# A transformer block on one core: h, the convolution's norm and its swish in half tiles, with the gate dots, diagonal blocks and last store rearranged

## The chip, the cores and the metric

One core of a Trainium2 chip runs the whole block as one program. The metric is device time in microseconds from launch to end. TensorE (PE) does the matrix products, VectorE (DVE) and ScalarE (ACT) the elementwise work, GpSimd (POOL) a little of it, and SyncE (SP) issues most transfers between the chip's memory and the on-chip buffer SBUF; POOL issues the rest. PE writes its results into eight banks of a second buffer, PSUM. Each engine works through its own queue in a fixed order; engines wait for one another through semaphores.

## The reference

One layer on a sequence of 1024 positions with 1024 channels, in float32:

```python
h = rmsnorm(x, pre_mix_g) * (1.0 + sc1) + sh1          # sh, sc, ga: rows of silu(c) @ ada_w + ada_b
proj = h @ w_in                                        # 1024 -> 1024 (glu) + 1536 (q, k, v) + 2048 (gates)
u = u_val * sigmoid(u_gate)
u = causal_depthwise_conv(u, conv_w, conv_b)           # 31 taps, 512 channels
u = silu(layernorm(u, conv_ln_g, conv_ln_b))
y_conv = u @ w_conv_out
y_att = stick_breaking_attention(q, k, v) @ w_att_out  # 8 heads of 64, strictly causal
merged = sigmoid(g_conv) * y_conv + sigmoid(g_att) * y_att
x = x + ga1 * rmsnorm(merged @ w_o, post_mix_g)
h = rmsnorm(x, pre_ffn_g) * (1.0 + sc2) + sh2
gate, up = split(h @ w_ffn_in)
x = x + ga2 * rmsnorm((silu(gate) * up) @ w_ffn_out, post_ffn_g)
```

## The kernel before

Activations are kept with channels on the 128 partitions and positions along the row, so a matrix of 1024 x 1024 is eight tiles of 128 x 1024. A product in full precision is made from three products of rounded parts: each operand is split into hi (rounded) and lo (the remainder), and PE computes hi·hi + hi·lo + lo·hi. The hi part is an ACT copy, the lo part a DVE subtraction. PSUM banks hold 128 x 512, so the positions are worked in two column halves, c = 0 and 1 (the slices hs).

The program runs through these stages.

*Start.* x is normed and modulated to h; its 16 tiles hhi and hlo (pool hp, 16 slots of 128 x 1024) are written by hi_op and lo_op. The order of ACT and DVE here is written out by hand (pin).

*Attention.* Four calls of attend, each for two heads. head works in blocks of 256 positions, four to a head (c from 0 to 3). For each it makes scores z on PE, sigmoids on ACT (ka, be), a product scan along the row on DVE, then transposes the probabilities on PE into the bank tr, four of 128 x 128 per bank. In a diagonal block (jp == c) one of the four is zero, and a tile of zeros is transposed for it. ACT copies tr into ahi, DVE makes alo, and PE multiplies both with v. The heads have a higher priority; other work fills PE's queue between their steps: the projections for q, k and v, the gated input of the convolution (glu, which writes u, a tile with one slot, and stores it to v_d), and the convolution (conv, which loads v_d into ph, makes 40 small products into the banks pcv, and stores to u_d).

*Gates.* Two of the eight pairs of gate tiles are plain products (the list PLAIN, four products). For the other six (GPAIRS) the product is made by a scheme with seven instead of eight half-size products. It needs sums and differences of quarters of h, the forms T1 to T4, built from f = hhi + hlo; B11, B21 and B22 are quarters of h itself. Two of a pair's seven products need only B11 and B21 and are made first, into the banks k1 and k2, stored as e_d and s_d (tiles e); other_five makes the other five.

*Norm.* ln_all loads u_d into cr, four tiles that take slots of hp, and does the layer norm over 512 channels, one column half after the other; then sigmoid, scaling and product give csil, which is split into chi and clo.

*Merge.* y_conv multiplies chi, clo with w_conv_out and with the gate. Beside it ada2_dots loads sixteen rows of the conditioning matrix and dots each with cb on DVE (dot_c). Then the attention's output, o_d, goes through w_att_out and its gate, the two branches are added, and the sum is split into mhi and mlo.

*Output projection, feed-forward, end.* These follow, and only the last step of them is touched: finish, called for the last quarter with last = ka, multiplies by the root rs and the gate, adds x1 (tiles xr) and stores four tiles.

A scheduler orders the instructions of each engine by priority and by its own estimate of times; tc.high_priority(offset) raises the priority of what stands in it. A tile of a pool waits for the former holder of its slot. The functions load and store issue the transfer on SP's and on POOL's queue. gemm is a product over banks of both column halves, load_w loads and splits a weight tile, banks2 takes two of the three banks of the pool main, and bkg takes turns over seven banks.

Of the kernel before, what the change touches and what calls it, by code (L numbers as in the profile page):

```python
# [18 lines left out]
P = 128  # L19
D = 1024  # L20
# [25 lines left out]
LN_PRI = 100  # L46
LN_DVE0 = (0, 1)
# [28 lines left out]
def tile_block(ctx: ExitStack, tc: tile.TileContext, xT, vecs, ada1, ada2, win, wv, wcv, wat, wo, w1, w2, cvw, out):  # L76
# [8 lines left out]
    hp = mkpool(ctx, "hp", 16)  # L85
# [125 lines left out]
    with ExitStack() as s0:  # L211
# [100 lines left out]
        def hi_op(k, cols=slice(0, T)):  # L312
            act.activation(hhi[k][:, cols], xs[k][:, cols], AF.Identity, bias=shift_of(k), scale=1.0)

        def lo_op(k):
            dve.scalar_tensor_tensor(hlo[k], xs[k], shift_of(k), hhi[k], op0=ALU.add, op1=ALU.subtract)
# [17 lines left out]
        for k in range(KT):  # L334
            hhi.append(hp.tile([P, T], F32R, tag="act", name=f"hhi{k}"))
            hlo.append(hp.tile([P, T], F32R, tag="act", name=f"hlo{k}"))
# [81 lines left out]
    with ExitStack() as sC:  # L418
        pc = mkpool(sC, "pc")
        with ExitStack() as sA:  # L420
# [25 lines left out]
            def conv(ct):  # L446
# [4 lines left out]
                for hf in range(2):  # L451
# [15 lines left out]
                    load(u_d[ct][hf * (NG // 2):(hf + 1) * (NG // 2)].rearrange("g p m -> p g m"), o)  # L467
# [53 lines left out]

            def head(p, hh, qst, kst, klo, vts, oT):
# [6 lines left out]
                for ci, c in enumerate(order):  # L529
# [5 lines left out]
                    for sc in range(nsc - 1, -1, -1):  # L535
# [27 lines left out]
                        for jp in range(min(c, 2 * sc + 1), 2 * sc - 1, -1):  # L563
                            tr = pst.tile([P, CH], F32, tag="tr", name=f"tr{tag}_{c}_{jp}")
                            for jj in range(2):
                                j = 2 * jp + jj
                                for ii in range(2):
                                    jo = (j - 4 * sc) * P
                                    src = zeros if (jp == c and jj == 1 and ii == 0) else probs[ii][:, jo:jo + P]
                                    o = jj * 256 + ii * P  # L570
                                    pe.transpose(tr[:, o:o + P], src, ident)  # L571
                            ahi = pa.tile([P, CH], F32R, tag="ahi", name=f"ahi{tag}_{c}_{jp}", bufs=2)
                            alo = pa.tile([P, CH], F32R, tag="alo", name=f"alo{tag}_{c}_{jp}", bufs=2)
                            act.activation(ahi, tr, AF.Copy)  # L574
                            dve.tensor_tensor(alo, tr, ahi, op=ALU.subtract)  # L575
                            for jj in range(2):
                                j = 2 * jp + jj
                                lhs = vts[j][:, hidx].rearrange("p a d -> p (a d)")
                                cols = slice(jj * 256, jj * 256 + 256)
# [22 lines left out]
            v = v_half(0)  # L602
            for p in range(4):
                glu(p)
                if p == 2:
                    v = v_half(1)
# [3 lines left out]
            conv(3)  # L610
# [1180 lines left out]
```

## Time and profile before

| | us |
|---|---|
| median of 3 runs | 1417.07 (1415.29 to 1421.37) |
| profiled execution | 1416.81 |
| its span, first to last instruction | 1415.0 |
| PE busy | 1383.6 |
| DVE busy | 1060.4 |
| ACT busy | 651.3 |
| POOL busy | 96.7 |

The span is the time from the first to the last instruction that the profiler saw; the run's time has a little on both sides of it. "Busy" is the time in which at least one instruction of the engine was under way. In a row of the profile, a line number such as L571 is that of the kernel before as printed above; "out<-in" are the names of tiles without their numbers; and an entry in square brackets is the idle time of the engine ahead of that instruction, with what ended it. In a row of waits the three numbers are the total in us, how often, and the longest. In a row of a group of instructions they stand as count, busy us, mean ns of one, and idle us ahead of them. In a row of transfers they are count, size, and the median time from issue to landing.

### The profile page before, as it was taken

What the parts mean: (1) busy time and instruction counts of PE and PEld (TensorE: products, weight loads), DVE (VectorE), ACT (ScalarE), POOL (GpSimd) and SP (SyncE); (2) the same over time, 40 slices, a digit from 0 to 9 for tenths busy, and PEclk for the clock granted to TensorE, in tenths of its full rate; (3) what the DMA queues carried; (4) which work ended last, traced back from release to release, by engine and by line L of the source; (5) the groups of instructions that cost most, each with busy time, mean ns of one, the idle gap of its engine ahead of it and who ended that gap; (6) DMA issues with size and microseconds to landing.
All of it is one profiled execution on the core that took longest, in us unless ns stands there. A gap on an engine that the chain in (4) does not pass through costs nothing.

```text
span 1415.0 us, 18809 instructions
## 1 busy us (share of the span) xinstructions
PE 1383.6 (98%) x6886; PEld 1156.1 (82%) x6886; DVE 1060.4 (75%) x1602; ACT 651.3 (46%) x1136; POOL 96.7 (7%) x183
## 2 busy tenths in 40 slices
PE   7999999999999999999999999999999999999996
PEld 4798898898888878888877778888888887888886
DVE  6898598576767789779588878778877775775357
ACT  5375465364553447412356553334444453334441
POOL 0000000000001110000012100001111110000000
PEclk8999999999999999999999999999999999999998
DMA  9112041131253645784935545456777769588833
GB/s 382 74 37 75 30 141 54 45 114 66 77 177 111 228 179 175 280 277 137 361 120 173 185 147 173 157 173 228 242 255 246 259 245 392 170 333 280 281 116 119
DMA packets 91116, 258.73 MB, mean 183 GB/s; under 512 B 9744, under 2 KB 20112, under 8 KB 90000
## 3 DMA queue, kind: packets, MB, share of 16 engines
q1 hardware_dynamic: 75088, 202.99, 42.1%
q0 software_dynamic: 15936, 54.54, 10.3%
q8 instruction: 54, 0.88, 0.3%
q14 instruction: 38, 0.31, 0.1%
HBM read 190.91 MB, written 66.58 MB: 182 GB/s over the span
## 4 chain that ended last, share of the span: by engine, by line
PE 80%; DVE 6%; issue 6%; DMA 5%; ACT 2%; POOL 1%; SPq 0%; DVEq 0%; POOLq 0%; ACTq 0%
PE ka L958 12%; PE ka L1500 8%; PE kc L958 7%; PE pwo L881 6%; PE pb L1500 4%; PE pgv L180 3%; PE pg L180 3%; PE pyc L180 3%; PE pya L180 3%; PE pv L481 3%; PE pcv L461 3%; PE tr L571 2%; PE pq L180 2%; PE pgg L180 2%; PE pk L180 2%
## 5 line engine op out<-in xcount | busy, mean ns | idle before, releaser
L559 DVE TENSOR_TENSOR_SCAN ka<-ka 128x128 f32<-128x128 f32 (+2 forms) x96 | 91.4, 968 | 22.8 <-ACT ka L555 22.5
L555 ACT ACTIVATE ka<-z 128x128 f32<-128x128 f32 (+2 forms) x96 | 47.1, 496 | 58.8 <-PE z L554 34.4
L575 DVE TENSOR_TENSOR alo<-tr,ahi 128x512 fp32r<-128x512 f32 x80 | 53.2, 685 | 18.2 <-ACT ahi L574 17.5
L1500 PE MATMUL ka<-gt,w2f 128*128 128x512 f32 x264 | 63.4, 390 | 0.8 <-DMA w2f<-w_d 0.8
L574 ACT ACTIVATE ahi<-tr 128x512 fp32r<-128x512 f32 x80 | 46.3, 601 | 38.1 <-PE tr L571 25.8
L561 DVE TENSOR_TENSOR be<-be,ka 128x127 f32<-128x127 f32 (+2 forms) x96 | 53.4, 573 | 9.6 <-ACT be L556 4.9
L1500 PEld LDWEIGHTS ka<-gt,w2f 128*128 128x128 f32 x264 | 49.4, 188 | 11.5 <-issue 1.4
L1066 PE MATMUL ke<-b,w_hi 128*128 128x512 f32 x176 | 55.2, 394 | 0.0
L135 DVE SCALAR_TENSOR_TENSOR ada<-ada,cb 128x1024 f32<-128x1024 f32 x32 | 38.8, 1223 | 20.7 <-DMA ada<-in_ada_dram 20.6
L556 ACT ACTIVATE be<-z 128x128 f32<-128x128 f32 (+2 forms) x96 | 46.2, 495 | 9.5 <-PE tr L571 9.3
L571 PE MATMUL tr<-ident,be 128*128 128x128 f32 x288 | 47.8, 273 | 0.4 <-DVE alo L575 0.4
L580 PE MATMUL av<-ahi,vst 128*128 128x256 f32 x160 | 44.2, 292 | 0.0
L461 PE MATMUL pcv<-ph,cvw 128*128 128x128 f32 x320 | 42.5, 276 | 0.8 <-DMA ph<-v_d 0.8
L581 PE MATMUL av<-alo,vst 128*128 128x256 f32 x160 | 42.8, 293 | 0.0
L461 PEld LDWEIGHTS pcv<-ph,cvw 128*128 128x128 f32 x320 | 39.5, 192 | 1.5 <-issue 1.2
L1066 PEld LDWEIGHTS ke<-b,w_hi 128*128 128x128 f32 x176 | 33.0, 188 | 7.8 <-issue 1.0
L481 PE MATMUL pv<-wv_hi,hhi 128*128 128x256 f32 x128 | 36.8, 288 | 2.1 <-DVE qst L505 1.4
L159 ACT ACTIVATE gt<-X 128x512 fp32r<-128x512 f32 x33 | 20.4, 630 | 39.5 <-DVE X L1543 12.4
L481 PE MATMUL pv<-wv_hi,hlo 128*128 128x256 f32 x128 | 36.7, 287 | 0.0
L481 PE MATMUL pv<-wv_lo,hhi 128*128 128x256 f32 x128 | 36.4, 285 | 0.0
L551 PE MATMUL z<-kst,qst 128*128 128x256 f32 (+2 forms) x96 | 36.2, 382 | 0.0
L571 PEld LDWEIGHTS tr<-ident,be 128*128 128x128 f32 x288 | 34.7, 140 | 1.8 <-PE z L554 0.5
(533 smaller groups left out, 4097.7 us busy)
## 6 DMA issues: line engine op xcount, KB each, us to landing
w_d<-w2o POOLq DMA_DIRECT2D x44, 512.0 KB, 8.0
w2f<-w_d SPq DMA_DIRECT2D x44, 512.0 KB, 5.4
ada<-in_ada_dram SPq DMA_DIRECT2D x32, 512.0 KB, 6.1
w2r<-in_w_dram SPq DMA_DIRECT2D x44, 256.0 KB, 3.8
w1g<-in_w_dram SPq DMA_DIRECT2D x21, 512.0 KB, 3.6
w1u<-in_w_dram SPq DMA_DIRECT2D x21, 512.0 KB, 5.2
cvw<-in_cvw_dram SPq DMA_DIRECT2D x20, 512.0 KB, 3.7
ada_w<-in_ada_dram SPq DMA_DIRECT2D x8, 1024.0 KB, 12.0
```

Of the source, the lines that this page charges most:

```text
L180: pe.matmul(bank, st[:, cols], mv[k][:, c * CH:(c + 1) * CH], start=(i == 0 and s == 0), stop=(i == n - 1 and s == 2))
L461: pe.matmul(cv[:, gi * TM:(gi + 1) * TM], wts[n][:, at:at + P], ph[:, g, SH - 1 - d:SH - 1 - d + TM], start=(d == 0), stop=(d == SH - 1))
L481: pe.matmul(pv[:, :256], st[k][:, tcols], mv[:, wc], start=(k == 0 and i == 0), stop=(k == KT - 1 and i == 2))
L555: act.activation(kap[:, s_lo:s_hi], z[:, zo:zo + w], AF.Sigmoid, bias=0.0, scale=-0.125)
L559: dve.tensor_tensor_scan(rev, rev, rev, init, op0=ALU.mult, op1=ALU.bypass)
L561: dve.tensor_tensor(beta[:, :m], beta[:, :m], kap[:, s_lo + 1:s_lo + 1 + m], op=ALU.mult)
L571: pe.transpose(tr[:, o:o + P], src, ident)
L575: dve.tensor_tensor(alo, tr, ahi, op=ALU.subtract)
L881: pe.matmul(bank_, st[:, cols], mv[k][:, cs], start=(k == 0 and q == 0), stop=(k == KT - 1 and q == 2))
L958: pe.matmul(bank_, st[:, cols], t[:, mv], start=(first and j == 0 and s == 0), stop=(j == HK - 1 and s == 2), skip_group_check=not first)
L1066: pe.matmul(kbs[f], wes[f][st][:, cols], t[:, mv], start=(i == 0 and j == 0 and q == 0), stop=(j == HK - 1 and q == 2), skip_group_check=i ...
L1500: pe.matmul(dst, w[st][:, cols], g[mv], start=first and s == 0, stop=last and s == 2, skip_group_check=more)
```

## The change

The change has these parts.

- h, in place of 16 tiles of 128 x 1024, is written as 32 half tiles of 128 x 512 in three kinds of slots: the second column half of its first four channel tiles (kind 0, 8 slots), the first column half of these (kind 1, 8 slots), and both halves of the other four (kind 2, 16 slots). hi_op, lo_op and the building of f work in halves.
- The norm of column half c (ln_half) takes slots of kind c, with priorities 1000 and 600; it stands behind the gates in the program, and before them by its priority. Swish, chi and clo are half tiles too; clo takes slots of kind 2. After y_conv the slots are given back, and 16 whole ones are opened for the merge.
- The early products of the gate pairs are made for two pairs at a time, and B21's accumulates in the bank of B11's; the DVE addition between them goes.
- In a diagonal block three transposes are made, not four. The zero quarter lies in two pairs of tiles (diag_t) that are set to zero once; the order of the quarters is turned so that the zero one comes first.
- The sixteen dots of ada2_dots go from y_conv into attention: 6, 5 and 5 behind the first three calls of glu, each loaded on POOL's queue into the slot of u.
- conv stores to u_d on POOL's queue, and the last conv stands behind the first plain gate.
- The last tile of the merge is worked in column halves at a raised priority (LASTM).
- In the last call of finish, ACT copies three of four tiles of x1 into PSUM ahead, POOL does one of the four output tiles, DVE works on pairs of rows at once, and the stores go out in the order 2, 3, 0, 1, pinned.

```diff
+    def half(kind, name, dt=F32):
+        return hq.tile([P, CH], dt, tag=f"half{kind}", name=name, bufs=(8, 8, 16)[kind])
...
         def lo_op(k):
-            dve.scalar_tensor_tensor(hlo[k], xs[k], shift_of(k), hhi[k], op0=ALU.add, op1=ALU.subtract)
+            for cs in hs:
+                dve.scalar_tensor_tensor(hlo[k][:, cs], xs[k][:, cs], shift_of(k), hhi[k][:, cs], op0=ALU.add,
+                                         op1=ALU.subtract)
...
-            hhi.append(hp.tile([P, T], F32R, tag="act", name=f"hhi{k}"))
-            hlo.append(hp.tile([P, T], F32R, tag="act", name=f"hlo{k}"))
+            kind = (1, 0) if k < KT // 2 else (2, 2)
+            hhi.append(halves(kind, f"hhi{k}", F32R))
+            hlo.append(halves(kind, f"hlo{k}", F32R))
...
-                    load(u_d[ct][hf * (NG // 2):(hf + 1) * (NG // 2)].rearrange("g p m -> p g m"), o)
+                    store(u_d[ct][hf * (NG // 2):(hf + 1) * (NG // 2)].rearrange("g p m -> p g m"), o)
...
+                                    if on and jj == 1 and ii == 0:
+                                        continue
...
+                            if on:
+                                ahi, alo = diag_t[next(ndiag) % 2]
+                                used = slice(P, CH)
...
+            def ada2_dots(n):
+                for _ in range(n):
+                    col = a2.popleft()
+                    w = pc.tile([P, D], F32, tag="u", name=f"ada2_{col}", bufs=1)
+                    store(w, ada2[col - 2 * KT])
+                    dot_c(w, cb, col)
+
             for p in range(4):
                 glu(p)
+                ada2_dots((6, 5, 5, 0)[p])
...
-            conv(3)
             for n in PLAIN:
+                if n == PLAIN[1]:
+                    conv(3)
...
+            for i0 in range(0, len(GPAIRS), 2):
+                two = GPAIRS[i0:i0 + 2]
+                ek, a12 = {}, {}
+                for i in two:
+                    raw = wp.tile([P, T], F32, tag="wraw", name=f"ew{i}")
+                    load(raw, win[20 + 2 * i])
+                    ek[i] = bank(f"k1_{i}")
+                    prod0(ek[i], w_op(f"a11_{i}", raw[:, :CH], act, dve), "B11")
+                    a12[i] = w_op(f"a12_{i}", raw[:, CH:], act, dve)
+                    e0 = sgp.tile([P, CH], F32, tag="sg", name=f"ee0_{i}", bufs=2)
+                    act.activation(e0, ek[i], AF.Copy)
+                    store(e_d0[i], e0)
+                for i in two:
+                    prod0(ek[i], a12[i], "B21", False)
+                    e1 = sgp.tile([P, CH], F32, tag="sg", name=f"ee1_{i}", bufs=2)
+                    act.activation(e1, ek[i], AF.Sigmoid, bias=0.0, scale=1.0)
+                    store(s_d[2 * i][:, :CH], e1)
...
+        def ln_half(c):
+            s0_, s1_, mean, sq = (half(c, f"l{nm}{c}") for nm in ("s0", "s1", "mean", "sq"))
+            cr = [half(c, f"cr{ct}_{c}") for ct in range(CONVT)]
+            for ct in range(CONVT):
+                load(cr[ct], channels(u_d[ct])[:, c * CH:(c + 1) * CH])
+            dve.tensor_tensor(s0_, cr[0], cr[1], op=ALU.add)
...
+                for oh in range(NCH):
+                    ms = slice(oh * mh, (oh + 1) * mh)
+                    dve.tensor_tensor(o.t[oh].rearrange("p (m r) -> p r m", r=PH)[:, c * r2:(c + 1) * r2],
+                                      ar[:, :, ms], sr[:, :, ms], op=ALU.mult)
...
-            if q == LN_AT:
-                with tc.high_priority(offset=LN_PRI):
-                    ln_all()
+        cr = {}
+        for c, prio in ((0, 1000), (1, 600)):
+            with tc.high_priority(offset=prio):
+                cr[c] = ln_half(c)
+        with tc.high_priority(offset=300):
+            csl = [halves((c, c), f"csil{ct}") for c in range(NCH) for ct in (2 * c, 2 * c + 1)]
+            for ct in range(CONVT):
+                silu(ct, cr, csl[ct])
...
+            if last:
+                xp = {}
+                for mm_ in (2, 3, 1):
+                    xp[mm_] = bank(f"x1p{mm_}").rearrange("p (a b) -> p a b", a=2)
+                    act.activation(xp[mm_], xrs[c, mm_][:, :, cols], AF.Copy)
             rstd_from(rs, m, a, ps_sum, D)
+            if last:
...
+                pool.tensor_tensor(y0, y0, r2, op=ALU.mult)
+                pool.tensor_tensor(y0, y0, xrs[c, 0][:, :, cols], op=ALU.add)
+                for m, y in ((2, y2_), (3, y3)):
+                    for i in range(2):
+                        dve.scalar_tensor_tensor(y[:, i], last[2 * (m - 2) + i][:, cols],
+                                                 gpost2[:, 2 * m + i:2 * m + i + 1], rs, op0=ALU.mult, op1=ALU.mult)
+                    add(dve, y, y, xp[m])
+                    put(m, y)
+                dve.tensor_tensor(y1, y1, r2, op=ALU.mult)
+                add(dve, y1, y1, xp[1])
+                put(0, y0)
+                put(1, y1)
```

171 lines of the change are left out of this document (94 added, 77 removed).

## The prediction

> **What bounds the kernel now.** I read the page first, then the sums over stretches of time, then PE's waits, then single moments.
>
> ```profile
> span 1415.0 us, 18809 instructions
> PE 1383.6 (98%) x6886; PEld 1156.1 (82%) x6886; DVE 1060.4 (75%) x1602; ACT 651.3 (46%) x1136; POOL 96.7 (7%) x183
> PE 80%; DVE 6%; issue 6%; DMA 5%; ACT 2%; POOL 1%; SPq 0%; DVEq 0%; POOLq 0%; ACTq 0%
> ```
>
> The profiled execution took 1416.81 us, 1.81 us more than its span and 0.26 us less than the median 1417.07 of the three runs. PE is busy for 98% of the span: whatever does not shorten PE's own work, its gaps, or the end after its last matmul moves nothing. Stage by stage (attention; gates with the convolution's norm; merge):
>
> ```profile
> core 0: us, PE busy (x) PEld busy (x) DVE busy (x) ACT busy (x) POOL busy (x), PEclk, DMA share, GB/s
> 107.00:432.00 325.00, 323.87 (x2019) 284.43 (x2018) 231.65 (x326) 172.41 (x355) 7.13 (x7) 1.00 0.28 88
> 457.00:513.00 56.00, 54.56 (x235) 43.43 (x233) 41.44 (x66) 26.78 (x49) 8.64 (x16) 1.00 0.62 211
> 513.00:570.00 57.00, 56.10 (x240) 44.94 (x241) 54.55 (x81) 39.23 (x54) 6.00 (x12) 1.00 0.53 180
> 588.00:666.00 78.00, 78.00 (x346) 64.61 (x345) 66.45 (x98) 17.17 (x17) 0.54 (x1) 1.00 0.68 233
> ```
>
> In attention PE lacks 1.13 us of 325, in the merge nothing; in the gates 1.44 and 0.90 us, while DVE is at 54.55 of 57 in the second gate stretch. PE's waits between 350 and 600 us are these six, 3.6 us together:
>
> ```profile
> PE ka L415 <- DVE gv L703: 1.2, 1, 1.2
> PE kc L415 <- DVE gw L705: 0.8, 1, 0.8
> PE pcv L461 <- DMA ph<-v_d: 0.8, 1, 0.8
> PE tr L571 <- DVE alo L575: 0.4, 1, 0.4
> PE kc L415 <- DVE s1o L402: 0.2, 1, 0.2
> PE ka L415 <- DVE s2o L402: 0.2, 1, 0.2
> ```
>
> A wait costs a little more than its gap. Matmuls of 512 columns start 78.00 / 346 = 0.225 us apart (the merge's row above), so behind the two of the first row below the next was due at 511.85 + 0.45 = 512.30. It starts at 513.70: 1.40 us lost for a gap shown as 1.16, part of it the first matmul's longer start. I add 0.17 us to each wait.
>
> ```profile
> 511.85 0.68 PE L415 MATMUL kc<-T1o,s1o 128*128 128x512 f32 x2
> 513.70 3.06 PE L415 MATMUL ka<-T3o,s3o 128*128 128x512 f32 x12 [1.16 <-DVE gv L703]
> ```
>
> **The change, part by part.**
>
> *Diagonal transposes.* Each of the 8 heads has 4 diagonal blocks, each with one transpose of zeros; the change takes these 32 out and lets two kept tiles hold the zeros.
>
> ```profile
> L571 PE MATMUL tr<-ident,zeros x32: 270/273/279, 84.9 to 417.6; 128*128 128x128 f32 x32
> 404.19 0.27 PE L571 MATMUL tr<-ident,zeros 128*128 128x128 f32 x1
> 404.30 0.71 PE L571 MATMUL tr<-ident,be 128*128 128x128 f32 x5
> ```
>
> 273 ns is the time through the array; what one occupies is the distance to the next start, 404.30 - 404.19 = 0.11 us. 32 x 0.11 = 3.5 us off an engine that lacks 1.13 us of its stage: -3.5. ACT's and DVE's ops on these blocks also shrink from 512 to 384 columns; neither is on the path, so 0.
>
> *conv(3) behind the first plain gate.* PE waited 0.8 us for the convolution's input, ph. With a gate of 48 matmuls (48 x 0.23 = 11 us) ahead of it the load has landed: -(0.8 + 0.17) = -1.0. Its stores go from SP's queue to POOL's; POOL is busy 7.13 us in 325, so 0. If the gate runs dry elsewhere the 1.0 stays: ends 0 and -1.0.
>
> *Gates and norm.* The four remaining DVE waits are 1.2 + 0.8 + 0.2 + 0.2 = 2.4 us, with 4 x 0.17 = 3.1 us. What is DVE doing when PE waits? It waits itself, for the norm's loads, with gate work queued behind:
>
> ```profile
> 497.21 0.69 DVE L734 TENSOR_TENSOR la<-cr,cr 128x512 f32<-128x512 f32 x1 [3.88 <-DMA cr<-u_d]
> 499.76 0.69 DVE L736 TENSOR_TENSOR la<-la,cr 128x512 f32<-128x512 f32 x1 [1.26 <-DMA cr<-u_d]
> ACT ee L629 <- DVE ee L628: 17.7, 5, 7.6
> ```
>
> Before, the slots for cr come free only when the early gate products have read h's first column half. The half norm takes slots of the second half, which nothing reads after the B-forms are built, so its loads go out tens of us earlier and DVE does some 17 of its 512-wide ops (17 x 0.61 = 10 us, step from the L741 row below) in a stretch where it is at 41.44 of 56. The early products' two halves accumulate in one bank, which drops 6 DVE adds (L628) and ACT's 17.7 us of waits for them. So I take all of it: -3.1; ends 0 and -3.1. The swish on DVE, already strided, keeps its element count:
>
> ```profile
> L760 DVE TENSOR_TENSOR csil<-cr,csig 128x1024 f32<-128x1024 f32 x4 | 8.7, 2178 | 0.0
> ```
>
> 16 quarters of 0.54 us make the same 8.7 us: 0.
>
> *h in halves at the start.* The lo op is split eight times; at 0.69 us for 512 columns against
>
> ```profile
> L316 DVE SCALAR_TENSOR_TENSOR hlo<-x,mod,hhi x8: 1278/1280/1283, 28.2 to 59.7; 128x1024 fp32r<-128x1024 f32 x8
> ```
>
> that is at most 8 x (2 x 0.69 - 1.28) = 0.8 us more DVE work, while the first half is ready 0.6 us sooner. Ends +0.8 and -0.6, taken as 0.
>
> *The sixteen gate dots.* They go from the merge into attention, and their loads from SP's queue to POOL's, through the single slot of u.
>
> ```profile
> L135 DVE SCALAR_TENSOR_TENSOR ada<-ada,cb 128x1024 f32<-128x1024 f32 x16 | 19.3, 1222 | 6.9 <-DMA ada<-in_ada_dram 6.9
> DVE ka L559 <- ACT ka L555: 21.0, 20, 2.9
> DVE alo L575 <- ACT ahi L574: 17.0, 12, 5.8
> ```
>
> In the merge their leaving frees 19.3 us of DVE, worth 0, since PE misses nothing there; for the same reason the finer last merge step is 0. In attention DVE rises from 231.65 to 251 of 325. A dot waits in DVE's queue for its load (6.9 us over 16, here), and behind it wait scans and products of the heads. Ends: 0, if other PE work covers it, and +6.9, if none does. Two rows alone hold 38 us of DVE waits in the same stage, against which PE lost 1.13 us, so I take a value near the covered end: +1.2, a sixth.
>
> The Trainium skill, page "DMA: Bandwidth & Descriptors", section "Anatomy of one DMA", fits a POOL-issued transfer as 2.0 us plus bytes over 436 GB/s: an estimate of 3.2 us for these 512 KB, and by it the dots would find their data and the term would be 0. The rows further down (6.1 and 8.0 us) speak for the longer time, so the sum keeps +1.2.
>
> *The end.* rs is ready at 1405.8; then DVE works alone:
>
> ```profile
> 1405.83 1.43 DVE L1637 TENSOR_TENSOR yc<-yc,frs 128x256 f32<-128x256 f32 x4
> 1407.18 1.65 DVE L1640 SCALAR_TENSOR_TENSOR yc<-ka,gpost,frs 128x256 f32<-128x256 f32 x4
> 1408.75 2.76 DVE L1540 TENSOR_TENSOR yc<-yc,xr 128x256 f32<-128x256 f32 x8
> 506.95 2.49 DVE L741 TENSOR_TENSOR cr<-cr,lm 128x512 f32<-128x512 f32 x4
> L169 POOL TENSOR_TENSOR wv_lo<-wv_raw,wv_hi 128x1024 fp32r<-128x1024 f32 x2 | 5.5, 2759 | 47.0 <-ACT wv_hi L159 47.0
> ```
>
> 1405.83 to 1411.51 is 5.7 us. After: the same four L1640 ops (1.65) and four 512-wide ops at 2.49 / 4 = 0.62 (2.5): 4.15. POOL does y0 meanwhile, two ops of 512 at 2.76 / 2 = 1.4: 2.8 us, inside it. Three copies of x1 into PSUM are ready long before, on an ACT that is idle. Gain 5.7 - 4.15 = -1.5. If POOL's ops did not shrink with the tile, 2 x 2.76 = 5.5, y0's and so y1's store would start where the last one does now: 0. Ends 0 and -1.5; I take -1.5.
>
> **Sum:** -3.5 - 1.0 - 3.1 - 1.5 + 1.2 = -7.9, from 1416.81: 1408.9, and 1409.2 from the median; I say 1409.0.
>
> **The rivals.**
>
> *The gates' waits come back.* DVE is nearly full in 513 to 570, and a norm put ahead of the gates can delay a gate's operand as well as before. Against it: the dropped adds, and slack in 457 to 513. Without the 3.1: 1412; with as much again in new waits: 1415. That is no change within what a measurement of this kernel can tell, about 0.5% or 7.1 us.
>
> *The loads cost nothing* (the page's rule as a mechanism: every dot finds its data, the heads never wait, and the 0.4 us wait in attention goes too): 1408.9 - 1.2 - 0.6 = 1407.1.
>
> *Slower: u's slot.* u of the second glu needs the slot that six load-and-dot turns use one after another.
>
> ```profile
> 126.47 0.33 SPq L104 DMA_DIRECT2D v_d<-u  x1
> 187.35 2.01 DVE L443 TENSOR_TENSOR u<-pgv,sg 128x512 f32<-128x512 f32 x2
> v_d<-u SPq DMA_DIRECT2D x4, 512.0 KB, 2.9
> ada<-in_ada_dram SPq DMA_DIRECT2D x32, 512.0 KB, 6.1
> w_d<-w2o POOLq DMA_DIRECT2D x44, 512.0 KB, 8.0
> Y<-g_d SPq DMA_DIRECT2D x11, 512.0 KB, 12.9
> L107 POOL DMA_DIRECT2D s_d<-sg x8 | 4.5, 561 | 64.2 <-ACT sg L616 64.2
> SPq L104 <- DVE u L443: 78.3, 4, 27.6
> ```
>
> From the landing of the first u's store (126.5 + 2.9 = 129.4) to the second u at 187.35 are 58 us, 9.7 per turn. A turn is a landing, the dot's 1.2 and 0.56 for POOL's issue: 7.9 us at 6.1, 9.8 at 8.0, 14.7 at 12.9. While a load waits for the slot, POOL's queue holds what follows it, the convolution's stores among it. In the last case u is 6 x 5.0 = 30 us late, its two banks are held, fillers lack banks, and SP's queue, which already waits for u up to 27.6 us, holds the weights behind it. If PE loses two thirds, 20 us: 1429. It decides from about 9.7 + 15 / 4 = 13.5 us per turn, where the 7.9 and 7.1 more are gone. For it: the single slot. Against: DMA is at 0.28 in this stage, and half of the loads behind the 6.1 were made in the merge, at 0.68.
>
> **How the numbers follow.** Forecast 0.58, of which 0.48 ends under 1410.0 (0.5% under the median) and 0.10 above; gates' waits back 0.22, all within 0.5%; loads free 0.07, faster; u's slot 0.13, of which 0.12 ends over 1424.2. Faster 0.55, same 0.33, slower 0.12. The low end takes every gap and the start's 0.6 as gains, and a further us for gaps that the trace shows only as late starts: 1407.1 - 0.6 - 1 = 1405.5. The high end takes the gates' case with its new waits, 1415, and 1 us of the dots' larger end: 1416. The forecast's own range is 1406 to 1412.
>
> **What would show it.** Right: 6854 matmuls, none from zeros; cr loads issued before 480 us and no DVE wait for cr ahead of a gate; PE's waits for gv and gw gone; attention's PE gap still near 1 us; under 4.5 us of DVE between rs and the last output store. Wrong: DVE waits for ada loads in attention with PE gaps behind them; u of the second glu later than 187 us; a new PE wait for s1o, s2o or chi at the gates; POOL's y0 ending after DVE's y1.

## The result and the profile after

The changed kernel takes 1438.81 us (median of four runs, 1435.91 to 1442.87), the kernel before beside it 1416.18: a ratio of 1.0163, with a 95% interval from 1.0143 to 1.0184. It is 23 us slower; the prediction was 1409.0, with 1416.0 as the upper end of its range. The profiled execution took 1441.67 us. The four runs are two near 1436 us and two near 1442, the profiled one among the slower, and a piece of chance in the start stage, told below, is about that large.

The page of the changed kernel (span; busy time, share and instructions of each engine):

```profile
span 1439.9 us, 18760 instructions
PE 1404.0 (98%) x6854; PEld 1161.1 (81%) x6854; DVE 1054.2 (73%) x1625; ACT 655.6 (46%) x1159; POOL 113.1 (8%) x209
```

PE makes 32 matmuls fewer, as the change says (6854 against 6886), and is busy for 20.4 us more (1404.0 against 1383.6). So the time did not go into gaps first of all: the same matmuls take longer. The sums over the stretches that were shown of before, and over one in the feed-forward part:

```profile
core 0: us, PE busy (x) PEld busy (x) DVE busy (x) ACT busy (x) POOL busy (x), PEclk, DMA share, GB/s
107.00:432.00 325.00, 323.71 (x2025) 283.31 (x2024) 246.50 (x364) 168.93 (x356) 20.49 (x30) 1.00 0.32 105
513.00:570.00 57.00, 53.82 (x231) 42.83 (x231) 53.16 (x91) 37.42 (x60) 5.94 (x11) 1.00 0.39 133
588.00:666.00 78.00, 78.00 (x340) 63.56 (x339) 42.58 (x54) 17.60 (x18) 1.62 (x3) 1.00 0.42 143
836.00:1185.00 349.00, 348.33 (x1503) 281.43 (x1503) 273.97 (x437) 145.10 (x254) 46.34 (x86) 1.00 0.60 208
```

The last stretch in the kernel before:

```profile
836.00:1185.00 349.00, 348.10 (x1532) 286.78 (x1530) 270.43 (x432) 145.79 (x255) 46.91 (x87) 1.00 0.65 227
```

This is the row to learn from. The change touches nothing between 836 and 1185 us. PE is busy for the same 348 of 349 us at a granted clock of 1.00 in both, and gets 1503 matmuls done in place of 1532: one starts every 232 ns in place of 228. A busy share can't show this; the count beside it does. The merge has the same sign (340 against 346 in 78 us, both with PE busy throughout).

Laid side by side, the two profiled executions part in three places. PE's first product for pgv starts 11.1 us later than before (117.60 us against 106.46), its last group of products 22.0 us later (1423.94 against 1401.94), and the span ends 24.9 us later. So 11.1 us arise in the start stage, 10.9 between the start and the last products, and 2.9 behind them.

PE's longest new waits (us in total, times, longest):

```profile
PE pv L502 <- ACT wv_hi L176: 2.3, 1, 2.3
PE ka L436 <- DVE gw L760: 1.9, 2, 1.7
PE pv L502 <- DVE klo L540: 1.5, 1, 1.5
PE ka L436 <- ACT s2o L176: 1.2, 1, 1.2
```

The second and the fourth are at the gates, 3.1 us together: the waits that were to go are back under other names. The first and the third are at the end of the start stage, at the first v products. The kernel before waits there too, for 2.1 us, but in the changed kernel the waits are longer and are followed by a time at half clock, which the kernel before does not have there (changed kernel first, then before):

```profile
72.50:77.50 5.00, 1.19 (x5) 0.59 (x4) 3.88 (x7) 4.92 (x7) 0.00 (x0) 0.96 0.00 0
77.50:84.00 6.50, 6.10 (x28) 5.81 (x28) 6.32 (x9) 5.70 (x9) 0.00 (x0) 0.51 0.52 161
```

```profile
72.50:77.50 5.00, 5.00 (x42) 4.83 (x41) 4.41 (x8) 4.92 (x7) 0.00 (x0) 1.00 0.34 105
77.50:84.00 6.50, 5.83 (x47) 5.17 (x46) 4.90 (x11) 3.52 (x12) 0.00 (x0) 1.00 0.30 83
```

PEclk is 0.51 from 77.5 to 84 us. One thing in this pair is chance. From 22 to 44 us PEclk is 0.53 in the changed kernel and 0.77 in the one before: a time at half clock of 20.5 us and one of 10.2. Which of the two comes is not the kernel's doing: the changed kernel with its pool moved by 128 bytes, with the same instructions, had the short one, and the kernel before with its pool moved the long one. Ten more us at half clock cost up to 5 us; of these, 3.9 are left at the first v product, which starts at 75.27 us in the changed kernel and at 71.39 in its moved twin. So the medians below are read, and beside them stretches of the trace that leave the start out.

The end: POOL's two operations on y0, DVE's first and last behind rs, and the closing instructions of POOL and SP (count, shortest, median and longest in ns, first and last start):

```profile
1428.02 1.26 POOL L1710 TENSOR_TENSOR yc<-yc,frs 128x512 f32<-128x512 f32 x1 [220.00 <-issue]
1429.36 1.26 POOL L1711 TENSOR_TENSOR yc<-yc,xr 128x512 f32<-128x512 f32 x1
1427.83 0.88 DVE L1714 SCALAR_TENSOR_TENSOR yc<-ka,gpost,frs 128x256 f32<-128x256 f32 x2
1431.57 0.69 DVE L1606 TENSOR_TENSOR yc<-yc,x1p 128x512 f32<-128x512 f32 x1
L1879 POOLq DRAIN  x3: 40/93/9808, 1429.3 to 1439.6; - x3
L1879 SPq DRAIN  x3: 7/7/7, 1435.0 to 1439.4; - x3
```

DVE needs 1427.83 to 1432.26, 4.4 us in place of 5.7, near the predicted 4.15, and y0 is done inside it. SP, which has issued the stores, is through at 1435.0. But POOL closes with an instruction of 9.8 us, which the profile starts with POOL's last operation at 1429.3; 8.5 us of it lie behind that operation's end (1429.36 + 1.26 = 1430.62), and the program ends behind it at 1439.9. The kernel before has that instruction too, early, where it costs nothing:

```profile
L1786 POOLq DRAIN  x3: 40/93/8429, 1185.9 to 1414.8; - x3
L1786 SPq DRAIN  x3: 7/7/7, 1414.2 to 1414.5; - x3
```

From DVE's first operation behind rs to the end of the span are 12.1 us after and 9.2 before: the end is 2.9 us longer, not 1.5 shorter. SP's row says what was lost. In the kernel before SP's first closing instruction stands 0.8 us ahead of the end (1414.2, 1415.0). With the same 0.8 us behind 1435.0 the changed kernel would have ended at about 1435.8, which is 8.0 us behind DVE's first operation and 1.2 us better than before. That is an estimate from these rows; no run shows it.

### The profile page after: what moved, and what is told of

Same layout as the page of the kernel before. It is cut to its first block, busy times and chain, and to the rows that moved or that the text cites. A ratio compares the mean times of both kernels' runs of the same rounds, so it can differ in the third digit from the quotient of the medians.

```text
span 1439.9 us, 18760 instructions
## 1 busy us (share of the span) xinstructions
PE 1404.0 (98%) x6854; PEld 1161.1 (81%) x6854; DVE 1054.2 (73%) x1625; ACT 655.6 (46%) x1159; POOL 113.1 (8%) x209
## 4 chain that ended last, share of the span: by engine, by line
PE 85%; DVE 5%; issue 4%; DMA 4%; ACT 1%; POOL 1%; SPq 0%; POOLq 0%; DVEq 0%; ACTq 0%
PE ka L1024 14%; PE kc L1024 8%; PE ka L1566 8%; PE pwo L947 6%; PE pb L1566 4%; PE pv L502 3%; PE pyc L197 3%; PE pgv L197 3%; PE pg L197 3%; PE pya L197 3%; PE pgg L197 2%; PE pq L197 2%; PE pk L197 2%; PE kb L1024 2%; PE pa L1566 2%
## 5 line engine op out<-in xcount | busy, mean ns | idle before, releaser
L1566 PEld LDWEIGHTS ka<-gt,w2f 128*128 128x128 f32 x264 | 49.4, 188 | 12.1 <-issue 1.9
L585 ACT ACTIVATE be<-z 128x128 f32<-128x128 f32 (+2 forms) x96 | 46.7, 493 | 10.9 <-PE tr L602 10.8
L611 DVE TENSOR_TENSOR alo<-tr,ahi 128x512 fp32r<-128x512 f32 x48 | 32.2, 684 | 13.3 <-ACT ahi L610 12.7
L610 ACT ACTIVATE ahi<-tr 128x512 fp32r<-128x512 f32 x48 | 28.3, 601 | 28.4 <-PE tr L602 25.6
L176 ACT ACTIVATE s1o<-s 128x512 fp32r<-128x512 f32 x22 | 13.9, 630 | 54.6 <-PE ka L1024 43.7
L176 ACT ACTIVATE gt<-X 128x512 fp32r<-128x512 f32 x33 | 20.4, 629 | 40.3 <-PE ka L1566 13.1
L1132 PE MATMUL ke<-b,w_lo 128*128 128x512 f32 x88 | 34.6, 394 | 1.4 <-DVE w_lo L1066 1.4
```

Of the source, the lines that this page charges most:

```text
L585: act.activation(beta[:, :w], z[:, zo:zo + w], AF.Sigmoid, bias=0.0, scale=0.125)
L1132: pe.matmul(kbs[f], wes[f][st][:, cols], t[:, mv], start=(i == 0 and j == 0 and q == 0), stop=(j == HK - 1 and q == 2), skip_group_check=i ...
L1566: pe.matmul(dst, w[st][:, cols], g[mv], start=first and s == 0, stop=last and s == 2, skip_group_check=more)
```

## The experiments

Ratios are to runs of the kernel before on the same chip, with 95% intervals. The rows were run on several chips, on which the medians of the kernel before lie between 1414.71 and 1416.18 us; so where two rows are compared below, their ratios are compared too. The cuts from the kernels have their constants written out, and comments added.

| kernel | us | ratio to before |
|---|---|---|
| changed kernel | 1438.81 | 1.0163 [1.0143, 1.0184] |
| before, h's pool moved by 896 bytes | 1438.25 | 1.0149 [1.0116, 1.0182] |
| changed, y0 on DVE | 1436.65 | 1.0142 [1.0115, 1.0169] |
| changed, pool moved by 128 bytes | 1425.33 | 1.0074 [1.0046, 1.0102] |
| both of these | 1422.52 | 1.0051 [1.0038, 1.0064] |
| and the last start block in order | 1420.20 | 1.0031 [1.0019, 1.0044] |
| and the gate dots in the merge | 1417.50 | 1.0016 [1.0008, 1.0025] |
| and (dots in attention) the swish behind s2o | 1416.10 | 1.0006 [0.9995, 1.0017] |
| all five | 1412.96 | 0.9979 [0.9969, 0.9989] |
| all five, last conv ahead of the gate | 1415.43 | 1.0002 [0.9990, 1.0014] |
| before, h's first ops in halves | 1427.29 | 1.0089 [1.0071, 1.0108] |
| before, no transposes of zeros | 1420.37 | 1.0037 [1.0024, 1.0051] |
| and the merge's banks turned by two | 1413.31 | 0.9989 [0.9980, 0.9997] |
| and the last conv behind the plain gate | 1415.43 | 1.0000 [0.9990, 1.0010] |

**Where do the 5 ns come from?** The change opens the pool of h, and later that of the merge, on the other side of SBUF (side="right"), which the list of its parts does not name. Slow are the matmuls of 512 columns whose moving row, the operand that streams past the weights, lies in that right-hand pool. At full clock, and with the next one close behind, 2651 of them start 232.8 ns apart on average, and the other such matmuls of the changed kernel 227.7. In the kernel before all of them start 227.2 ns apart. By the addresses in the built programs, h's pool started at byte 56416 before and the weights' at 19552, both 96 modulo 256; in the changed kernel the right-hand pool starts at 163808, which is 224. A program of its own, with nothing of the block's work in it, runs groups of 48 matmuls between one weight tile and one long row and moves the start of one of them by 32 bytes from group to group.

```diff
+    for i in range(64):
+        last = run("v", i, 512, 8 * i, 0, 48)       # moving row starts 32 bytes later each time
+    for i in range(64):
+        last = run("h", i, 256, 8 * i, 0, 48)       # the same with 256 columns
+    for i in range(16):
+        last = run("s", i, 512, 248, 8 * i, 48)     # the weight tile's start moves
```

> A program of its own, not the block: one fp32r weight tile against rows of 512 columns (groups va to cl: 64 starts, 32 bytes apart), then of 256 columns (groups beginning with h), 48 matmuls each, then 16 starts of the weight tile (groups beginning with s). Theory A, the place of the moving row: the pace depends on where the row starts within 2048 bytes; groups starting at 2016 of 2048 (number 59) take about 0.233 us per matmul, at 1120 (number 31) 0.227. Theory B, what runs beside it (other engines or transfers writing to the same memory): nothing runs beside it here, so all 64 starts take 0.227 us. Theory C, the address region or the side of the memory: the same flat 0.227, since all lies at the low end.

Its timeline; vaa, vab, vac, vai have the moving row at 128, 160, 192 and 128 modulo 256, and the weights at 128. In sah and sap the weights are at 96, in saa at 128, and the row at 96 in all three:

```profile
35.38 11.04 PE L102 MATMUL vaa<-x,w 128*128 128x512 f32 x48
46.26 11.37 PE L102 MATMUL vab<-x,w 128*128 128x512 f32 x48
57.46 11.16 PE L102 MATMUL vac<-x,w 128*128 128x512 f32 x48
68.46 11.37 PE L102 MATMUL vad<-x,w 128*128 128x512 f32 x48
124.49 11.05 PE L102 MATMUL vai<-x,w 128*128 128x512 f32 x48
135.38 11.37 PE L102 MATMUL vaj<-x,w 128*128 128x512 f32 x48
1112.64 11.36 PE L102 MATMUL saa<-x,w 128*128 128x512 f32 x48
1190.83 11.05 PE L102 MATMUL sah<-x,w 128*128 128x512 f32 x48
1279.89 11.04 PE L102 MATMUL sap<-x,w 128*128 128x512 f32 x48
```

From start to start over 48: (46.26 - 35.38) / 48 = 226.7 ns for vaa, (57.46 - 46.26) / 48 = 233.3 for vab, 229.2 for vac, 226.9 for vai. So the pace depends on where row and weights stand to one another modulo 256 bytes: equal 226.7, the row 64 bytes ahead 229, every other multiple of 32 bytes 232 to 234. Each offset of the row was run eight times and agrees within 0.2 ns, and moving the weights gives the same figures. The theory had a period of 2048 bytes, which was wrong; that nothing else ran shows it isn't contention, and that one pool holds fast and slow starts shows it isn't the side. With 256 columns there was no such difference: all starts lie between 117.8 and 119.9 ns, the equal ones among the slower.

The same made in the kernel before, where no instruction and no order changes, only the addresses:

```diff
+    mkpool(ctx, "padp").tile([P, 224], F32, name="pad")     # 896 unused bytes ahead of hp
     hp = mkpool(ctx, "hp", 16)
```

> The kernel before with 896 unused bytes per partition ahead of the pool hp; every instruction and its order stay, and only the tiles above move by 896 bytes, from 1120 to 2016 of 2048. Theory A (place of the row): the 4618 matmuls of 512 columns from these tiles go from 227 to 233 ns, +26 us: 1440 to 1446. Theory C (side or region): the tiles stay on their side and within 1 KB of their place, no change, 1413 to 1420. Theory D (the change's own waits made it slow): no change either.

Measured: 1438.25, 22 us slower than before, a little under the 1440 to 1446 of theory A. An unused tile alone makes the kernel before as slow as the changed one. The stretch in the feed-forward part:

```profile
836.00:1185.00 349.00, 348.46 (x1497) 281.27 (x1496) 273.28 (x436) 144.61 (x251) 45.84 (x85) 1.00 0.61 208
```

And taken back in the changed kernel:

```diff
+    mkpool(ctx, "padp", side="right").tile([P, 32], F32, name="pad")   # h now at 96 modulo 256
     sH = ctx.enter_context(ExitStack())
```

> The kernel after with 128 unused bytes at the end of the right side, so that h and the tiles that follow it start at 1888 of 2048 and not at 2016; nothing else changes. Theory A, if the place within 256 bytes decides (2016 and 1888 differ there, 224 against 96, and 96 is the kernel before's): the 14.5 us of slow matmuls go, 1421 to 1427. Theory A, if it is the nearness of a 2048-byte boundary: a part of it, or nothing. Theory C: no change, 1435 to 1443.

Measured: 1425.33, 13.5 us faster by the medians and 12.6 by the ratios, with 1529 matmuls in the same stretch. From PE's first product for pgv to its last group of products, which leaves out both the start and the end, the moved kernel takes 1294.5 us (113.14 to 1407.59), the changed one 1306.3 and the kernel before 1295.5. So the move takes back 11.9 us there, a little more than the 10.9 that the change had lost: the addresses are the largest part of the loss.

**The end.** y0's two operations go to DVE:

```diff
-                pool.tensor_tensor(y0, y0, r2, op=ALU.mult)
-                pool.tensor_tensor(y0, y0, xrs[c, 0][:, :, cols], op=ALU.add)
+                dve.tensor_tensor(y0, y0, r2, op=ALU.mult)
+                dve.tensor_tensor(y0, y0, xrs[c, 0][:, :, cols], op=ALU.add)
```

> The kernel after with the two operations on y0 in the last step on VectorE in place of GpSimd. If GpSimd's closing drain holds the end: the span after the last matmul goes from 15.8 to some 12.9 us (the drain's 4.2 us go, two operations of 0.62 us come), 2.9 us in all, and GpSimd's drain stays under 0.2 us. If the drain is only recorded long and the stores set the end: 1.2 us longer.

```profile
1423.70 0.69 DVE L1710 TENSOR_TENSOR yc<-yc,frs 128x512 f32<-128x512 f32 x1
L1879 POOLq DRAIN  x3: 40/93/10668, 1204.9 to 1432.7; - x3
```

Measured: 1436.65. That is 2.2 us less by the medians, which lie closer than the runs scatter; the trace decides. The long instruction stands at 1204.9 now, begun with POOL's last work, and the end from DVE's first operation (1423.70) to the span's 1432.9 is 9.2 us, just that of before. DVE's own work there is as long as before as well (1423.70 to 1429.46, 5.8 us for 5.7), so this run does not show what a shorter DVE end is worth. Both repairs together:

> The changed kernel with both repairs so far: 128 unused bytes so that the right-hand pool starts at the same place modulo 256 bytes as the weights, and y0 on DVE, which leaves POOL's drain at the end at 0.1 us. If the two costs are separate they add: 1425.3 - 2.2 = 1423.2 us, and 7 us over the kernel before remain, of which a theory S of the start (below) names 5.6. If the two share a cause, 1425.

Measured: 1422.52. Alone the two lower the ratio by 0.0089 and 0.0021, together by 0.0112: they add.

**The start.** In the kernel before ACT splits the first v weight ahead of q's copies; in the changed kernel it comes seventh, behind six copies of q and k (the first and the last of the six are shown):

```profile
66.08 1.06 ACT L159 ACTIVATE wv_hi<-wv_raw 128x1024 fp32r<-128x1024 f32 x1 [6.37 <-PE pq L331]
67.05 0.57 ACT L502 ACTIVATE qst<-pq 64x512 fp32r<-64x512 f32 x1
```

```profile
70.65 0.59 ACT L523 ACTIVATE qst<-pq 64x512 fp32r<-64x512 f32 x1 [10.15 <-PE pq L351]
73.67 0.59 ACT L537 ACTIVATE kst<-pk 64x512 fp32r<-64x512 f32 x1
74.17 1.04 ACT L176 ACTIVATE wv_hi<-wv_raw 128x1024 fp32r<-128x1024 f32 x1
```

The first experiment restores that order in the changed kernel, the second makes it wrong in the kernel before:

```diff
+                k_begin = len(nc.cur_bb.bb.instructions)
                 for b_, w_ in zip(ws, w0s):
                     gemm_k(b_, w_, k)
+                if k >= KT - 1:
+                    pin(k_begin, PINNED[:1])          # PE alone, k = 7
```

> The same, with PE's first products of the last of h's eight row blocks (k = 7, three weights by two columns halves by three terms) kept in program order. Theory S: halving h's first ops lets the left column half run ahead on PE, so that the first q weight's slot comes free 1.4 us later, ACT and DVE take q's and k's copies ahead of the split of the v weights, PE waits 4.3 us at the first v products instead of 2.1, and those waits are followed by 6.8 us at half clock. With the last block in order, ACT's and DVE's order is that of before (the v weights first): the waits are back at 2.1 us, no half clock between 70 and 84 us, 1423.2 - 2.2 - 3.4 = 1417.6 us. Rival: the half clock comes from something else that the change has at the start (the diagonal tiles' zeros, the place of the tiles): then about 1421 to 1423, with the window still there.

Measured: 1420.20, 2.3 us less, and 3.5 less between the two profiled executions. The half clock after 70 us is gone (PEclk 1.00 from 66 to 107) and the waits are back at 1.5 us, as theory S has it; but not all of its 5.6 us arrives. PE idles 4.4 us between 90 and 450 us where it idled 2.7 in the run before: part of the gain is given back in attention.

```diff
         def hi_op(k, cols=slice(0, T)):
+            for cs in (hs if cols.stop - cols.start == T else (cols,)):
...
         def lo_op(k):
+            for cs in hs:
```

> The kernel before with one part of the change: h's hi and lo ops are made in column halves, its tiles stay whole and at their place. Theory S: ACT's order at 65 to 76 us is the changed kernel's, PE's waits at the first v products are 4.3 us and the clock is at half for 6.8 us between 70 and 84: 1416.2 + 2.2 + 3.4 = 1421.8 us. The prediction's term for these halves was 0 (ends +0.8 and -0.6): 1416. Rival as above: the waits without the half clock, 1418.4.

Measured: 1427.29, where theory S had 1421.8. The first gate product starts 5.6 us later than before (462.61 against 456.99), as theory S has it. The rest is a wait that nobody had named, the first of these rows:

```profile
PE pwo L884 <- DVE sga L824: 3.8, 1, 3.8
PE pv L484 <- ACT wv_hi L159: 2.4, 1, 2.4
PE pv L484 <- DVE klo L522: 1.5, 1, 1.5
```

It is followed by 3.4 us at half clock (PEclk 0.89 from 670 to 675 us and 0.77 from 675 to 680), and 1421.8 + 3.8 + 1.7 is 1427.3. The next experiment shows where it comes from.

**The transposes alone.** In the kernel before, diag_t and the three transposes as in the change, nothing else:

> The kernel before with another part alone: the 32 transposes of zeros left out, two kept tile pairs hold the zeros. The prediction's term: 32 x 0.11 = 3.5 us, so 1412.7 us. Rival: what a transpose frees is taken by the next wait for ACT's and DVE's copies of the same block, as PE has some of its attention waits there: 1416.

Measured: 1420.37, slower. By the end of the merge PE is 2.9 us ahead of the kernel before (its last row starts at 662.53, there at 665.43); then:

```profile
667.03 0.47 PE L896 MATMUL pwo<-mhi,wo_hi 128*128 128x512 f32 x1 [3.88 <-DVE sga L836]
668.00:672.00 4.00, 4.00 (x12) 3.12 (x11) 2.45 (x4) 1.06 (x1) 0.00 (x0) 0.57 0.88 268
```

The first output projection waits for the PSUM bank of the last merge product. By the built programs it takes bank 0 in all of these kernels; the last merge product took bank 2 before and takes bank 0 here, as it does in the run with the ops in halves. That turn had moved by the scheduler's new order alone. The wait of 3.9 us is followed by 3.4 us at half clock, and at the last product of the output projection PE is 2.9 us behind the kernel before (757.67 against 754.80): 5.8 us lost at one bank. Not all of the slower time is seen in this trace: the runs' median is 5.2 us over the kernel before, the profiled execution, the fastest of six, 3.4. So the banks were turned on purpose:

```diff
+        for _ in range(2):
+            next(uidg)
         wa = None
```

> The kernel before with the 32 transposes of zeros out, as in the run that was slower than before by 5 us, and the merge's PSUM banks turned by two places, so that the first out-projection does not get the bank of the last merge product. Theory P: the transposes' gain was there (2.9 us ahead of the kernel before at the end of the merge) and was lost at that bank, 3.9 us of wait and 3.4 us at half clock; with the bank free the gain arrives at the end: 1415.2 - 2.9 = 1412.3 us. Rival: the gain is lost wherever PE meets the next wait: 1415 to 1420.

Measured: 1413.31, no PE wait there at all, and a ratio of 0.9989 [0.9980, 0.9997]: faster than the kernel before by 1.6 us (0.4 to 2.8). With the last conv behind the first plain gate:

> The same as the run before, and the last convolution behind the first plain gate. The prediction's term for that: PE's wait for ph, 0.8 us in the kernel before and 1.6 us with the transposes out, goes: 1412.3 - 1.6 - 0.2 = 1410.5 us; without a gain from it 1412.3.

Measured: 1415.43, no gain: 2.1 us more than without the move, with intervals that overlap. The wait for ph is gone, and PE waits for wg_hi (1.0) and for gw and gv (2.3, against 0.8 without the move).

**Dots and swish.** Both start from the changed kernel with three repairs. First the dots go back to where they stood before, beside y_conv:

> The changed kernel with the three repairs (128 bytes of shift, y0 on DVE, the last row block of the first products in order), and the sixteen gate dots taken back out of attention into the merge, where they stood before. Theory D: the dots are what makes PE idle for 4.4 us between 90 and 450 us, against 1.1 before (the prediction had 1.2 us for them); without them the idle time is back near 1.1 us: 1420.2 - 3.3 = 1416.9 us or a little less. The prediction's term: 1420.2 - 1.2 = 1419.0 us. Rival: the attention's new waits come from the new order of its own copies and scans, as in the kernel before with the transposes out, where PE idles 2.2 us there: 1420.

From 90 to 450 us, the changed kernel as it was; then the one with three repairs, with the dots in attention, and without:

```profile
90.00:450.00 360.00, 357.78 (x2234) 312.88 (x2233) 275.81 (x409) 189.20 (x398) 22.35 (x33) 1.00 0.32 105
```

```profile
90.00:450.00 360.00, 355.58 (x2185) 309.19 (x2184) 273.48 (x403) 187.53 (x391) 22.47 (x34) 1.00 0.33 107
DVE ada L154 <- DMA ada<-in_ada_dram: 20.0, 13, 3.3
```

```profile
90.00:450.00 360.00, 358.36 (x2211) 313.60 (x2210) 260.74 (x377) 190.05 (x396) 14.63 (x19) 1.00 0.27 87
```

PE idles 4.4 us with them and 1.6 without, and 2.2 in the changed kernel as it was. Measured: 1417.50, 2.7 us less by the medians, which are of two chips, and 2.1 by the ratios. In the second, the swish's sigmoid of the second column half goes behind s2o:

```diff
+                with tc.issue_after(split_of[GPAIRS[3 if c else 0]]):
+                    act.activation(sg, a, AF.Sigmoid, bias=b_, scale=g)
```

> The three repairs again, dots in attention, and one order changed at the gates: the swish's first sigmoid of the second column half is issued on ACT after the split s2o of the fourth gate pair, which stood behind it. Theory G: that sigmoid waits up to 3.9 us for the norm on DVE, s2o waits behind it, and PE waits 1.9 us for s2o, after which the clock is at half for 3.4 us (1.7 us lost): without it 1420.2 - 3.6 = 1416.6 us, and no half clock near 540 us. Rival: DVE is late by itself (it waits for a gate weight's load), PE waits as long for the next DVE result: 1420.

In the changed kernel ACT's queue reads:

```profile
534.35 1.52 ACT L807 ACTIVATE csig<-cr,vec 128x512 f32<-128x512 f32 x2 [2.59 <-DVE cr L798]
535.77 0.61 ACT L176 ACTIVATE s2o<-gs 128x512 fp32r<-128x512 f32 x1
```

The sigmoid waits for the norm on DVE, and s2o, which PE needs at once, stands behind it. Measured without that: 1416.10, 4.1 us less by the medians and 3.5 by the ratios; PE's waits between 455 and 600 us fall from 3.2 us to 0.9, and no half clock is left there.

**All five**, and then the last conv put back:

> The changed kernel with all five repairs: 128 bytes of shift, y0 on DVE, the last row block of the first products in order, the gate dots back in the merge, and the swish's sigmoid behind the fourth pair's s2o. If the pieces are separate, they add: 1417.5 - (1420.2 - 1416.1) = 1413.4 us, or 1414.71 - 1.3 against the kernel before on the same chip, so faster by 0.1%. If the dots' stalls and the gates' wait are partly the same delay (DVE late), about 1415 to 1416. If the prediction's other terms were right beside these five, 1409.

> The same with the last convolution back ahead of the first plain gate, as before the change. With the transposes out in the kernel before, moving the convolution replaced PE's wait for ph (1.5 us) by one for the gate's own weight, wg_hi (1.0 us): if that is all, this run is within 0.5 us of the one beside it. By the prediction's term (-1.0) it is 1 us slower; if the convolution behind the gate is what crowds DVE at the gates (waits for gw and gv of 2.3 against 0.8 us there), 1 to 2 us faster.

Measured: 1412.96, 0.2% faster than before (0.1 to 0.3). By the ratios the single repairs add up to 0.9991, and 0.9979 was measured: they add, within what the intervals can tell. With the conv ahead of the gate it is 1415.43, 2.5 us more, where the prediction's term was 1.0. No wait for ph is among PE's waits in that run; at the gates PE waits 3.0 us in it and 0.9 in the one beside it. This page is of the faster:

```profile
span 1409.7 us, 18766 instructions
PE 1380.0 (98%) x6854; PEld 1152.7 (82%) x6854; DVE 1054.4 (75%) x1627; ACT 654.9 (46%) x1159; POOL 101.8 (7%) x191
```

## Why the prediction was wrong, step by step

*What the sum left out.* No step asked where the tiles come to lie. The prediction read "78.00 / 346 = 0.225 us" as the price of a matmul, and that holds for this kernel's addresses only. Opening the pool on the other side of SBUF raised the price of 2651 matmuls by 5.6 ns: 14.8 us by the count, 12.6 to 13.5 by the run that takes it back. So the step that failed first is a cost that the sum held at nothing, without a reason: the move of the pool. This alone turns the sign. All three rivals were waits; none had this.

*The end, -1.5.* The mechanism on DVE was right (4.4 us for 4.15). The failing step is "POOL does y0 meanwhile ... inside it": it counted POOL's operations and not the closing instruction of 9.8 us that POOL begins with the last of them. The end became 2.9 us longer. DVE's saving was there to be had, some 1.2 us by the estimate from SP's row above, but the run with y0 on DVE gives it back together with POOL's close, so no run shows it.

*h in halves at the start, taken as 0.* The two ends (+0.8, -0.6) priced the durations of DVE's ops. What halves change is the order: PE takes the left column half ahead, a weight's slot is given back 1.4 us later, ACT and DVE copy q and k first, PE waits 2.2 us more and gets 6.8 us at half clock: +5.6 at the first gate product in the kernel before, +2.3 by the medians in the changed one.

*The gates, -3.1.* The rival "the gates' waits come back" came true: 3.1 us of waits in the profiled execution, where the kernel before had 2.4, and as the rival had it by "a norm put ahead of the gates". Half of the loads went out early, as said (four at 457.6 us; the other four only at 496.3). In the kernel with three repairs DVE was not the place, though; ACT's queue was, with a sigmoid that the change lets run early. With the sigmoid behind s2o the kernel is 3.5 us faster by the ratios and PE's waits at the gates are 0.9 us, under the 2.4 of before, so a part of the gain that the step named was there to be had. In the changed kernel itself 1.9 of the 3.1 us are waits for gw, which DVE makes; whether they have the same cause no run shows.

*The gate dots, +1.2.* The mechanism was right, and the size depends on what stands around it. In the changed kernel as it was, PE idles 2.2 us between 90 and 450 us, 1.1 more than before, which is near the term; with three repairs the dots cost 2.1 us by the ratios and 2.8 by PE's idle time. DVE waits 16.2 us for their loads in the first and 20.0 in the second. By the Trainium skill's page "DMA: Bandwidth & Descriptors", section "Anatomy of one DMA", the estimate for these loads was 3.2 us. The changed kernel's row has 3.9 on POOL's queue, nearer to that than to the 6.1 that the sum went by, and the dots still cost PE time:

```profile
ada<-in_ada_dram POOLq DMA_DIRECT2D x16, 512.0 KB, 3.9
```

*u's slot.* The rival did not come: u of the second glu starts at 197.75 us, 10.4 later than before, and PE as a whole was 11.1 us late already at 117.60.

*The transposes, -3.5.* Right in kind: 6854 matmuls, none from zeros. About half arrives: 1.9 us by the first gate product in the run with them alone, and 1.6 (0.4 to 2.8) at the end with the banks turned. PE's next waits take a part of the rest: it idles 2.1 and 2.2 us between 90 and 450 us in these two runs, and 1.1 in the kernel before. What takes the remainder is not shown.

*conv(3), -1.0.* The wait for ph goes and one for wg_hi comes. In the kernel before without the transposes the move gains nothing (2.1 us more by the medians); in the kernel with five repairs it is worth 2.5 us, but at the gates and not at ph, and why is not shown.

With all five causes removed, the dots among them, the change is worth 2.7 us, against 9.1 of the sum without the dots' 1.2. What it would be at other orders of ACT and DVE stays open, since each edit moves them.

## What to carry to other kernels

Count matmuls per microsecond in a stage that the change does not touch; if that has moved, look at addresses before waits, and keep weights and moving rows at the same place modulo 256 bytes when a pool is moved. Where a scheduler orders the queues, an edit's first price is the order it brings about elsewhere: one part tried alone gained 2.9 us and lost 5.8 at a PSUM bank that it never touches. Leave the last ten microseconds to engines that close quickly.

## What the runs showed of the hardware

- A matmul of 128 x 512 in this rounded format starts 226.7 ns after the one before it if row and weights start at the same place modulo 256 bytes, 229 if the row is 64 bytes ahead, and 232 to 234 at the other multiples of 32 bytes; with 256 columns no such difference shows (117.8 to 119.9 ns).
- POOL's closing instruction took 8.2 to 10.7 us in all fifteen traces of the block and began with POOL's last work; it is hidden when POOL stops that much earlier.
- The clock falls to half for 3.4 us or twice that after short waits of PE, and not after each. By the Trainium skill, page "TensorE: Matmul & The Clock Gate", section "What's actually happening", the gate looks at free-running windows of about 3.4 us and halves the clock after an idle one. The lengths agree: 3.9 us of wait were followed by 3.4 us. The condition does not: in the run with three repairs a wait of 1.9 us was enough, and in the run with only y0 on DVE a wait of 2.4 us was not. Cut each trace into stretches of 3.41 us, laid so that its half-clock times begin and end at the cuts. Then the first wait falls into one stretch, in which PE was busy for 1.55 us, and the next is at half:

```profile
543.82:547.23 3.41, 1.55 (x7) 0.88 (x6) 3.41 (x7) 2.27 (x4) 0.12 (x1) 1.00 0.76 228
547.23:550.64 3.41, 3.41 (x10) 2.64 (x9) 3.41 (x7) 0.63 (x1) 0.54 (x1) 0.50 0.43 162
```

The wait of 2.4 us is shared by two stretches, with 2.33 and 1.90 us of PE's work, and the clock stays:

```profile
533.84 0.72 PE L436 MATMUL ka<-T2o,s2o 128*128 128x512 f32 x2 [2.38 <-ACT s2o L176]
532.54:535.95 3.41, 1.90 (x7) 1.30 (x8) 3.41 (x7) 3.41 (x7) 0.00 (x0) 1.00 0.38 138
535.95:539.37 3.42, 3.42 (x17) 2.82 (x16) 3.42 (x7) 3.35 (x7) 1.08 (x2) 1.00 0.20 77
```

So in these traces a stretch in which PE idles for about half of the time is enough. Where the line lies is not sharp: 1.82 us of work in such a stretch were followed by half clock in the moved changed kernel, and 1.65 were not in the run without the transposes.
